# The mixer of an encoder layer: fp32 weight blocks against fp32r pieces in hand-ordered steps

## The chip, the cores and the metric

The kernel runs on one core of a Trainium2 chip. The metric is device time in microseconds (us), the median of three runs; a profiled execution of the same program supplies the trace. TensorE is called PE here, its weight loads PEld, VectorE DVE, ScalarE ACT, GpSimd POOL, and the queue that issues most transfers SP.

## The reference, cut to what matters

One layer over 256 tokens of width 2048. The mixer is everything up to `@ w_out`: a projection, a recurrent group (RWKV-7, both directions) and an attention group. The rest is a retrieval over 16384 single-neuron experts ("PEER").

```python
h = rmsnorm(x, norm1_w[l])
p = h @ w_in[l]                                  # 2048 x 5248
z_rwkv, q, k, v = jnp.split(p, IN_SPLITS, axis=-1)
y_rwkv = rwkv7_bidir(z_rwkv, ...)                # 16 heads x 64, delta-rule scans, two directions
y_attn = axial_gqa(q, k, v, q_norm_w[l], k_norm_w[l])   # 16 query heads, 4 key heads
x = x + jnp.concatenate([y_rwkv, y_attn], axis=-1) @ w_out[l]
x = x + peer_ffn(rmsnorm(x, norm2_w[l]), ...)    # queries, top-16 of 128 x 128 keys, all experts gated
out = rmsnorm(x, normf_w)
```

## The kernel before, in words

Activations stand transposed: 128 channels on the partitions, 256 tokens along the row. A block of weights is 128 input channels by 128 output channels, and a product of 2048 input channels is 16 matmuls into one PSUM tile `pj`.

The mixer and the rest use two ways of multiplying. The rest of the kernel (`query`, `up`, `down`) works in *pieces*. A piece is eight weight blocks (512 KB, tile `raw`); ACT rounds it to fp32r (`wH`), DVE or POOL subtracts to get what the rounding lost (`wL`), and PE multiplies the parts in the one-pass format fp32r. Pieces go through `load_piece`, `split_piece` and `go`, three pieces ahead of their use. There the instructions of each engine stand in the order in which the code issues them (`manual_schedule`).

The mixer before does not work that way. `proj` loads quarter blocks (`rw`, 256 KB) and multiplies them as plain fp32 with `xA`, the scaled tokens; `wout_block` does the same for the output projection, and `late` for its last part. Its order on the engines is set by a scheduler at build time from a list of parts, `ORDER`: U is the projection of a unit (four heads), P the operands of its scan (`prep`), I the inverse of 32 x 32 triangles (60 small DVE operations), M their merge on PE, C the scan's chain over four chunks, Q, K, V and A the attention, w the output projection. The operands go to DRAM (`D2`, `DV`) and come back as `PK` and `VV` for the chain.

So the program before is: first tokens, the mixer, eight `late` pieces, the queries and searches, and then the long stretch of `up` and `down` pieces.

Of the kernel before, what the change touches and what calls it, by code (L numbers as in the profile page):

```python
# [38 lines left out]
ORDER = ("U0 P0 U1 P1 U2 I0 P2 U3 Q4 M0 P3 V K Q0 Q3 A0 Q1 Q2 A1 W C0 I1 A2 M1 C1 A3 w2 w3 w0")  # L39
# [93 lines left out]

def body(tc, a, out, dbg={}):
    nc = tc.nc
    V, S, G, T = nc.vector, nc.scalar, nc.gpsimd, nc.tensor
# [51 lines left out]
    xy = actp.tile([128, 2, 16, 256], F, name="xy")  # L188
    xA, yA2 = xy[:, 0], xy[:, 1]
    yR, yT = yA2[:, 0:8], yA2[:, 8:16]  # L190
# [10 lines left out]

    stream = [pool("st")]

    def wload(src, n=4):
        raw = stream[-1].tile([128, n, 128], F, name="rw", bufs=8)
        nc.sync.dma_start(raw, src)
        return raw
# [26 lines left out]

# [7 lines left out]
    pss = bank("pt")[:, 0:2]  # L242
    pro = tc.tile_pool(name="pro", bufs=1, side="right")
    wp = pro.__enter__()
    xrs = [wp.tile([128, 4, 256], F, name="xr", bufs=4) for c in range(4)]
    for c in range(4):
        nc.sync.dma_start(xrs[c], a["xT"][:, 4 * c:4 * c + 4, :])
    nc.sync.dma_start(cst, a["cst"])
    for c in range(4):
        xr = xrs[c]  # L250
        tt(V if c < 2 else G, xA[:, 4 * c:4 * c + 4], xr,
           Pm("n1", 4 * c, 4)[:, :, None].to_broadcast([128, 4, 256]), OP.mult)
    for c in range(4):
        sq = wp.tile([128, 4, 256], F, name="xq", bufs=2)
        act(sq, xrs[c], AF.Square)
        sm = wp.tile([128, 256], F, name="xs", bufs=2)
        V.tensor_reduce(sm, sq.rearrange("p k t -> p t k"), axis=AX.X, op=OP.add)
        for b in range(2):
            mm(pss[:, b:b + 1], sm[:, b * 128:(b + 1) * 128], ones[:, 0:1], c + b == 0, c == 3)
    rstd = const.tile([128, 2, 1], F)  # L260
    rsqrt(wp, rstd[:, :, 0], pss, 2, 1.0 / 2048, 1e-6)
    psb = bank("pt")[:, :256]
    spread(psb, rstd.to_broadcast([128, 2, 128]))
    act(rstdb, psb)
    pro.__exit__(None, None, None)

    dr = pool("dr", 1, DRAM)
    ldp = pool("ldp", 1, side="right")
    rwc = pool("rwc", 1, side="right")
    at = pool("at", side="right")  # L270
    wk = pool("wk", 1)
    two = lambda p: p.rearrange("p (a b) -> p a b", a=2)

    def proj(n):
        p = pp.tile([128, 256], F, name="pj")
        for c in range(4):
# [5 lines left out]
    def headscale(pl, sq, scale, add, guard=None, tag="s2", bt="pr"):  # L282

        p = bank(bt)[:, :8].rearrange("p (b i h) -> p b i h", b=2, i=2)
        for b in range(2):
            for i in range(2):
                mm(p[:, b, i], sq[:, i, b * 128:(b + 1) * 128], bones[:, 0:128:64], b + i == 0, True)
        s1 = pl.tile([128, 8], F, name="s1")
        rsqrt(pl, s1, p.rearrange("p b i h -> p (b i h)"), 8, scale, add, guard)
        s2 = pl.tile([128, 8, 64], F, name=tag, bufs=2 if tag == "w2" else 1)  # L290
        V.tensor_copy(s2, s1[:, :, None].to_broadcast([128, 8, 64]))
        s2 = s2.rearrange("p (b i h) n -> p b i (h n)", b=2, i=2)
        p = bank(bt).rearrange("p (a b) -> p a b", a=2)
        for i in range(2):
            spread(p[:, i], s2[:, :, i])
        return p
# [958 lines left out]
```

## Time and profile before

| | us |
|---|---|
| median of three runs (2274.86 to 2278.29) | 2276.07 |
| profiled execution, its own time | 2277.42 |
| its span, first to last instruction | 2275.6 |
| mixer, from the first matmul with `xA` to the first `late` one | 14.1 to 635.5 |
| `late` pieces | 635.5 to 664.4 |
| queries, searches, experts, output | 664.4 to 2275.6 |

The span is what the trace covers; 1.8 us of the profiled time lie around it. PE is busy in 97% of the span, so the question in each stretch is what PE does there and at which clock, before what it waits for. A busy sum counts overlapping instructions once; the mean of one matmul contains its pipeline's depth, so the rate is read from starts, not from means.

### The profile page before, as it was taken

How to read it: one execution, taken by the hardware profiler on the slowest of the kernel's cores; microseconds unless marked ns; L12 is line 12 of the kernel's file. 1: busy time of each engine (PE TensorE's matmuls, PEld its weight loads, DVE VectorE, ACT ScalarE, POOL GpSimd, SP SyncE). 2: the span in 40 equal slices, each digit the busy share in tenths (PEclk: the TensorE clock that was granted, in tenths of full speed). 3: DMA queues.
4: the chain of work that ended last, by engine and by line, in shares of the span. 5: the costliest groups of instructions: out<-in, count | busy, mean ns of one | idle time of the engine just before them, and what ended most of it. 6: DMA issues, size and time to landing. Idle time of an engine off the chain costs nothing.

```text
span 2275.6 us, 33493 instructions
## 1 busy us (share of the span) xinstructions
PE 2214.7 (97%) x12790; PEld 1883.2 (83%) x12790; DVE 1223.4 (54%) x2556; ACT 961.8 (42%) x1479; POOL 823.6 (36%) x377
## 2 busy tenths in 40 slices
PE   7999799899999999999999999999999999999997
PEld 6888688787878889999888888888888888887886
DVE  3365875675367788887443352342533433456654
ACT  1121222323137755555544444444444444444443
POOL 0000000000027600000755555555555555556554
PEclk9999799699999999999999999999999999999999
DMA  5465364275455546666756666566566566676674
GB/s 196 148 188 174 127 196 146 82 240 174 138 183 170 174 160 221 213 209 215 240 189 205 203 194 209 190 203 212 187 211 205 185 211 205 194 229 212 207 209 133
DMA packets 188832, 431.50 MB, mean 190 GB/s; under 512 B 39680, under 2 KB 82304, under 8 KB 184448
## 3 DMA queue, kind: packets, MB, share of 16 engines
q1 hardware_dynamic: 177376, 409.96, 57.2%
q10 hardware_dynamic: 11296, 19.40, 2.5%
q8 instruction: 101, 1.65, 0.3%
q14 instruction: 59, 0.48, 0.1%
HBM read 391.55 MB, written 37.75 MB: 189 GB/s over the span
## 4 chain that ended last, share of the span: by engine, by line
PE 91%; DVE 5%; ACT 1%; DMA 1%; issue 1%; ACTq 0%; SPq 0%; DVEq 0%
PE pc L158 37%; PE pj L158 33%; PE pr L158 19%; PE pt L158 1%; DVE wL L164 1%; DVE oh L164 1%; ACT wH L161 0%; PE pr L532 0%; DMA VV<-V 0%; DVE pk L164 0%; DVE xy L164 0%; DVE hh L807 0%; DVE AK L164 0%; DVE h L164 0%; DVE rs L164 0%
## 5 line engine op out<-in xcount | busy, mean ns | idle before, releaser
L164 POOL TENSOR_TENSOR wL<-raw,wH 128x1024 fp32r<-128x1024 f32 x328 | 798.3, 2438 | 1018.5 <-ACT wH L161 1011.9
L161 ACT ACTIVATE wH<-raw 128x1024 fp32r<-128x1024 f32 x544 | 575.4, 1060 | 456.3 <-PE pc L158 282.8
L164 DVE TENSOR_TENSOR wL<-raw,wH 128x1024 fp32r<-128x1024 f32 x216 | 274.1, 1269 | 347.4 <-ACT wH L161 347.3
L158 PE MATMUL pr<-hh,wH 128*128 128x512 f32 x1152 | 409.3, 396 | 0.2 <-ACT wH L161 0.2
L158 PE MATMUL pj<-hh,wH 128*128 128x512 f32 x1152 | 408.0, 395 | 1.5 <-DVE hh L807 1.3
L158 PE MATMUL pc<-wH,aH 128*128 128x512 f32 x1024 | 406.7, 397 | 1.1 <-DVE acc L164 1.1
L158 PE MATMUL pc<-wH,aL 128*128 128x512 f32 x1024 | 404.8, 395 | 0.0
L158 PE MATMUL pc<-wL,aH 128*128 128x512 f32 x1024 | 402.0, 393 | 0.0
L158 PE MATMUL pj<-xy,rw 128*128 128x256 f32 x1664 | 382.6, 386 | 0.0
L158 PEld LDWEIGHTS pj<-xy,rw 128*128 128x128 f32 x1664 | 316.6, 193 | 49.6 <-issue 4.7
L158 PE MATMUL pr<-hh,wL 128*128 128x256 f32 x1152 | 323.1, 281 | 1.4 <-DVE wL L164 1.4
L158 PE MATMUL pj<-hh,wL 128*128 128x256 f32 x1152 | 322.1, 280 | 0.0
L158 PEld LDWEIGHTS pj<-hh,wH 128*128 128x128 f32 x1152 | 216.4, 188 | 48.4 <-DVE hh L807 2.0
L158 PEld LDWEIGHTS pr<-hh,wH 128*128 128x128 f32 x1152 | 217.2, 189 | 46.6 <-ACT wH L161 0.5
L158 PEld LDWEIGHTS pc<-wH,aL 128*128 128x128 f32 x1024 | 192.2, 188 | 48.3
L158 PEld LDWEIGHTS pc<-wL,aH 128*128 128x128 f32 x1024 | 192.3, 188 | 46.6
L158 PEld LDWEIGHTS pc<-wH,aH 128*128 128x128 f32 x1024 | 192.2, 188 | 46.1 <-DVE acc L164 1.5
L158 PEld LDWEIGHTS pr<-hh,wL 128*128 128x128 f32 x1152 | 217.2, 189 | 2.4 <-DVE wL L164 2.4
L158 PEld LDWEIGHTS pj<-hh,wL 128*128 128x128 f32 x1152 | 216.5, 188 | 0.4
L164 DVE TENSOR_TENSOR acc<-pc,acc 128x512 f32<-128x512 f32 x128 | 86.2, 688 | 131.6 <-PE pc L158 131.6
L504 POOL COPY vp<-zv 128x256 f32<-128x256 f32 x16 | 7.7, 482 | 307.2 <-PE pr L509 177.2
L161 ACT ACTIVATE gc<-pc 128x512 f32<-128x512 f32 x64 | 69.1, 1080 | 72.8 <-PE pc L158 72.8
(294 smaller groups left out, 1995.2 us busy)
## 6 DMA issues: line engine op xcount, KB each, us to landing
raw<-u SPq DMA_DIRECT2D x256, 512.0 KB, 4.1
raw<-v SPq DMA_DIRECT2D x256, 512.0 KB, 3.9
rw<-win SPq DMA_DIRECT2D x160, 256.0 KB, 2.8
PK<-D ACTq DMA_DIRECT2D x16, 1024.0 KB, 7.9
raw<-wpq SPq DMA_DIRECT2D x32, 512.0 KB, 4.3
gd<-gc SPq DMA_DIRECT2D x16, 1024.0 KB, 4.9
h<-gd SPq DMA_DIRECT2D x32, 512.0 KB, 6.9
D<-pk SPq DMA_DIRECT2D x16, 896.0 KB, 4.4
```

Of the source, the lines that this page charges most:

```text
L158: T.matmul(o, l, r, start=start, stop=stop, skip_group_check=True)
L161: S.activation(o, i, f, **kw)
L164: e.tensor_tensor(o, x, y, op=op)
L504: G.tensor_copy(vp[:, 1:5], c4(rev(zv[:, i], d)))
```

## The change

The mixer now works in the same pieces as the rest. Each piece is rounded on ACT and subtracted on DVE, and eight blocks cost 24 fp32r matmuls of 256 columns (`mm3`) instead of eight fp32 matmuls. The scheduler's order is replaced by one that is written out: a loop of steps. In a step the code issues first what the last step's piece left to do (`ends`), then one piece (`go(True)`: its rounding on ACT, its matmuls on PE), then one slice of every task (generators for heads, operands, inverses, bonuses, attention, chains), and at the end of the step the subtraction (`rest_pieces`). A task's slices are cut so that what one engine makes in a step is read by another in a later step. The last query blocks (32 to 37) and the gate's blocks stand behind the value blocks, and from there only every second step has a piece until all of them are used. Some work moves between engines: scalings and copies from DVE to ACT and POOL, the mask of the triangles to one operation ahead of the inverse.

```diff
+    def round_piece():
+        i = at_["split"]
+        H = stp.tile([128, 8, 128], R, name="wH", bufs=AHEAD + 1)
+        L = stp.tile([128, 8, 128], R, name="wL", bufs=AHEAD + 1)
+        act(H, raws[i])
+        hl[i] = (H, L)
+        at_["split"] += 1
+
+    def rest_pieces():
+        while at_["rest"] < at_["split"]:
+            i = at_["rest"]
+            H, L = hl[i]
+            tt(todo[i][2], L, raws.pop(i), H.bitcast(F), OP.subtract)
+            at_["rest"] += 1
...
+    def step(late=False):
+        now = list(ends)
+        ends.clear()
+        V.n = 0
+        for t in now:
+            next(t)
+        if late:
+            go(True)
+        for t in list(tasks):
+            tasks.remove(t)
+            if next(t, StopIteration) is not StopIteration:
+                tasks.append(t)
+            if V.n >= STEP:
+                break
+        tasks[:0] = now
...
-    def proj(n):
-        p = pp.tile([128, 256], F, name="pj")
-        for c in range(4):
-            W = wload(a["win"][n, :, 4 * c:4 * c + 4, :])
-            for k in range(4):
-                mm(p, W[:, k], xA[:, 4 * c + k], c + k == 0, c + k == 6)
-        return p
+    def x_block(n, c, evict):
+        def use(H, L):
+            if c == 0:
+                xp[n] = bank()[:, :256] if n == 24 else pj()
+            for k in range(8):
+                mm3(xp[n], H[:, k], L[:, k], xS[:, c + k, 0], xS[:, c + k, 1], c + k == 0, c + k == 15)
+            if c:
+                ends.append(evict(n, xp.pop(n)))
+        return from_rows(a["win"][n, :, c:c + 8, :]), use, V
...
-                V.tensor_scalar(sg, sg, 0.5, 0.5, op0=OP.mult, op1=OP.add)
-                V.tensor_scalar(av, av, 0.5, 0.5, op0=OP.mult, op1=OP.add)
+        G.tensor_scalar(sg, sg, 0.5, 0.5, op0=OP.mult, op1=OP.add)
+        G.tensor_scalar(av, av, 0.5, 0.5, op0=OP.mult, op1=OP.add)
+        G.tensor_scalar(a2, av, Pm("ka", j), ka1[:, j:j + 1], op0=OP.mult, op1=OP.add)
...
-    for q in ORDER.split():
-        parts[q[0]](int(q[1:] or 0))
+    tasks += [all_heads(), operand_tasks(), bonuses(), inverses(), reorder(), all_qk(), attend(), attended(), chains()]
+    slots = 0
+    while at_["use"] < NO or ("C", 1) not in done:
+        i = at_["use"]
+        ok = i < NO
...
+        if NX <= i < NA:
+            ok = "A" in done and bool(x2T)
+        elif NA <= i < NO:
+            ok = ("C", 0) in done
+        for u in range(2, 4):
+            if 8 + 12 * u < i < NX and ("P", u - 2) not in done:
+                ok = False
+        if NQ < i < NX and "at2" not in pools:
+            ok = False
+        slots += 1
+        if "at2" in pools and i < NX and slots % 2:
+            ok = False
+        step(ok)
+        rest_pieces()
```

In the order of the built program the loop has 129 steps. They are numbered from 1 here; 103 of them have a piece, and five pieces stand ahead of them. Two places show what moved.

On PE, inside the chain of the first two units; `VV`, `PK`, `X` and `N` are the chain's tiles, `zA`, `kW` and `pe` the attention's. Before, the scheduler laid groups of fp32 projection matmuls (`xy,rw`) between the slices:

```order
L158 MATMUL pr<-zA 128x256 x2
L158 MATMUL pr<-kW,zA 128x256 x2
L158 MATMUL pj<-xy,rw 128x256 x4
L158 MATMUL pc<-X,PK 64x64 x16
L376 MATMUL pr<-cst,pe 128x128 x4
L158 MATMUL pj<-xy,rw 128x256 x2
L158 MATMUL pr<-zA 128x256 x2
L158 MATMUL pj<-xy,rw 128x256 x6
L158 MATMUL pc<-VV,PK 64x64
L158 MATMUL pc<-PK,VV 64x64
```

In the changed program the same stretch, two steps of which the second has no piece, and the first rows of the next step's piece:

```order
L985 MATMUL pr<-cst,pe 128x128 x4
L177 MATMUL pr<-kW,zA_3716 128x256 x2
L177 MATMUL pc<-VV,PK 64x64 x16
L177 MATMUL pc<-PK,VV 64x64 x16
L177 MATMUL pt<-vA,pt 128x64 x4
L985 MATMUL pr<-cst,pe 128x128 x4
L177 MATMUL pr<-zA_3444,zA_3716 128x256 x2
L177 MATMUL pc<-VV,PK 64x64 x16
L177 MATMUL pj<-xy,wH 128x256 x2
L177 MATMUL pj<-xy,wL 128x256
```

The projection matmuls that lay between the slices now stand together, 24 at a time, and slices of two steps follow each other without one between them.

On DVE, inside the first inverse; the `h` rows are its small operations, `z` and `zv` belong to a projected block, `pk` to the scan's operands. Before:

```order
L164 TENSOR_TENSOR xy<-pr,zv 128x512
L164 TENSOR_TENSOR h_1545<-h_1545,h_1547 128x25x6
L164 TENSOR_TENSOR h_1547<-h_1545 128x168
L164 TENSOR_TENSOR h_1545<-h_1545,h_1547 128x24x7
L164 TENSOR_TENSOR h_1547<-h_1545 128x184
L164 TENSOR_TENSOR z<-pj,rstdb 128x256
L164 TENSOR_TENSOR h_1545<-h_1545,h_1547 128x23x8
L164 TENSOR_TENSOR h_1547<-h_1545 128x198
L408 SCALAR_TENSOR_TENSOR zv<-z,prm,zv 128x255
```

Now, with one step from the subtraction that ends the step before it to the operations of its operands:

```order
L149 TENSOR_TENSOR h_2479<-h_2477 128x198
L149 TENSOR_TENSOR h_2477<-h_2477,h_2479 128x9x22
L149 TENSOR_TENSOR wL<-raw,wH 128x1024
L149 SCALAR_TENSOR_TENSOR zr<-z,prm,zr 128x255 x2
L149 TENSOR_TENSOR pk_2661<-pc,cst 64x4x64
L149 TENSOR_TENSOR pk_2661<-pc,cst 128x4x64
L149 TENSOR_TENSOR pk_2661<-pc,cst 64x4x64
L149 TENSOR_TENSOR pk_2661<-pc,cst 128x4x64
L149 SCALAR_TENSOR_TENSOR cs_2945<-cst,sg_2809 128x256
L149 TENSOR_TENSOR av_2810<-kk,av_2810 128x256
L149 TENSOR_TENSOR a_2811<-zk,a_2811 128x256
```

A subtraction of 1024 columns (`wL<-raw,wH`) now stands in each step with a piece, and the inverse comes in groups of three pairs, one group a step.

## Rows read from the trace of the kernel before

**Rows 1.** Windows over the four stretches: busy us of each engine (instructions), clock, DMA, GB/s.

```profile
0.00:14.10 14.10, 1.70 (x8) 1.65 (x8) 9.06 (x13) 5.20 (x5) 4.94 (x6) 1.00 0.87 308
14.10:635.50 621.40, 593.31 (x4340) 505.10 (x4339) 349.70 (x967) 138.30 (x341) 20.30 (x40) 0.95 0.52 160
635.50:664.40 28.90, 28.76 (x136) 25.13 (x136) 17.90 (x28) 11.66 (x26) 3.71 (x2) 1.00 0.53 179
664.40:2275.60 1611.20, 1590.93 (x8308) 1351.33 (x8308) 846.74 (x1549) 806.68 (x1108) 794.60 (x330) 1.00 0.63 200
```

**Rows 2.** The page's chain that ended last, by engine.

```profile
PE 91%; DVE 5%; ACT 1%; DMA 1%; issue 1%; ACTq 0%; SPq 0%; DVEq 0%
```

**Rows 3.** The chain in order of time: start us, us, engine, line, instructions.

```profile
29.34 71.66 PE pj L158 x332
455.70 7.92 DMA VV<-V
1079.69 5.55 PE pj L158 x32
```

**Rows 4.** Timeline of PE in an `up` piece: start us, us, instruction.

```profile
1079.53 0.39 PE L158 MATMUL pj<-hh,wH 128*128 128x512 f32 x1
1079.76 0.28 PE L158 MATMUL pj<-hh,wL 128*128 128x256 f32 x1
1079.88 0.39 PE L158 MATMUL pj<-hh,wH 128*128 128x512 f32 x1
```

**Rows 5.** Groups of PE in the mixer, by form: busy us, mean ns, idle before.

```profile
L158 PE MATMUL pj<-xy,rw 128*128 128x256 f32 x1664 | 382.6, 386 | 0.0
L158 PE MATMUL pj<-rw,xy 128*128 128x256 f32 x64 | 15.1, 384 | 0.0
L158 PE MATMUL pr<-pk,AK 64*128 64x128 f32 x256 | 29.1, 332 | 11.2 <-DVE AK L164 11.2
L158 PE MATMUL pr<-tl,lo 96*128 96x256 f32 x64 | 18.5, 415 | 0.7 <-ACT pk L161 0.7
```

**Rows 6.** Windows of 4 us in the mixer; PEclk is the granted clock.

```profile
236.00:240.00 4.00, 0.00 (x0) 0.00 (x0) 3.84 (x10) 0.82 (x3) 0.95 (x1) 0.72 0.48 159
426.00:430.00 4.00, 4.00 (x14) 2.83 (x14) 2.75 (x8) 1.42 (x5) 0.00 (x0) 0.50 0.01 4
430.00:434.00 4.00, 4.00 (x14) 3.06 (x13) 0.00 (x0) 1.50 (x6) 0.00 (x0) 0.50 0.38 148
```

**Rows 7.** The page's groups of the roundings and of DVE's subtractions.

```profile
L161 ACT ACTIVATE wH<-raw 128x1024 fp32r<-128x1024 f32 x544 | 575.4, 1060 | 456.3 <-PE pc L158 282.8
L164 DVE TENSOR_TENSOR wL<-raw,wH 128x1024 fp32r<-128x1024 f32 x216 | 274.1, 1269 | 347.4 <-ACT wH L161 347.3
```

**Rows 8.** The page's group of one weight load.

```profile
L158 PEld LDWEIGHTS pj<-hh,wL 128*128 128x128 f32 x1152 | 216.5, 188 | 0.4
```

**Rows 9.** Timeline of DVE, neighbours that don't depend on each other.

```profile
258.24 0.41 DVE L164 TENSOR_TENSOR z<-pj,rstdb 128x256 f32<-128x256 f32 x1
258.57 0.48 DVE L408 SCALAR_TENSOR_TENSOR zr<-z,prm,zr 128x255 f32<-128x255 f32 x1
258.96 0.57 DVE L164 TENSOR_TENSOR Ld<-pr,cst 32x128 f32<-32x128 f32 x2
```

**Rows 10.** A POOL group of 256 columns with two operands.

```profile
L164 POOL TENSOR_TENSOR ks<-ks,av 128x256 f32<-128x256 f32 x8 | 7.6, 951 | 101.2 <-DVE av L164 101.2
```

**Rows 11.** DMA issues: KB each, median us from issue to landing.

```profile
PK<-D ACTq DMA_DIRECT2D x16, 1024.0 KB, 7.9
D<-pk SPq DMA_DIRECT2D x16, 896.0 KB, 4.4
```

**Rows 12.** Timeline of the start, ACT and PE.

```profile
5.72 1.06 ACT L161 ACTIVATE xq<-xr 128x1024 f32<-128x1024 f32 x1 [3.70 <-DMA xr<-xT]
14.25 2.05 PE L158 MATMUL pj<-xy,rw 128*128 128x256 f32 x4
```

**Rows 13.** Window over the first 57 us.

```profile
0.00:57.00 57.00, 44.60 (x199) 39.14 (x200) 20.90 (x42) 9.27 (x13) 4.94 (x6) 1.00 0.58 195
```

More of the change, by code (lines that the diff above doesn't have):

```diff
@@ L736, in body, with pj @@
[L736 to L738 removed]
+    def pj(w=256):
+        return pp.tile([128, w], F, name="pj")
+    two = lambda p: p.rearrange("p (a b) -> p a b", a=2)
+    stp = pool("st2")
     todo, raws, hl = [], {}, {}
[L742 removed]
+    at_ = {"load": 0, "split": 0, "rest": 0, "use": 0}
@@ L803, in use @@
                 act(sq[0][:, n % 4], x2(n), AF.Square)
[L804 removed]
+        return two_rows(m, 4), use, V
     def rest(n):
@@ new lines, in body, with operand_tasks @@
+    half, turn = set(), set()
+    fin = {}
+    def operand_tasks():
+        last = {}
+        for u in range(4):
+            while not (("head", u) in done and "tl" in done):
+                yield
+            for d in range(2):
+                los[u, d] = wk.tile([96, 2, 256], F, name=f"lo{d}")
+                nc.sync.dma_start(los[u, d], a["l2"][u][:, d::2])
+            for d in range(2):
+                for i in range(2):
+                    while i in last and last[i] not in half:
+                        yield
+                    last[i] = (u, i, d)
+                    tasks.append(operands(u, i, d))
+                    for _ in range(3):
+                        yield
@@ new lines, in body, with attend, attended @@
+    yA = {}
+    def attend():
+        while not ("at2" in pools and "V" in done and ("qk", 0) in done):
+            yield
+        for e in range(18):
+            g, hq = divmod(e, 4)
+            if e > 1:
+                values(e - 2)
+            if 0 < e < 17:
+                turned(e - 1)
+            if e < 16:
+                while ("qk", g) not in done:
+                    yield
+                scores(e)
+            yield
+    def attended():
+        for g in range(4):
+            while not (g in yA and yS):
+                yield
+            y = yA[g].rearrange("p b a n -> p b (a n)")
+            p = two(bank())
+            for j in range(2):
+                for b in range(2):
+                    T.transpose(p[:, j, b * 128:(b + 1) * 128], y[:, b, j * 128:(j + 1) * 128], ident)
+            s = slice(8 + 2 * g, 10 + 2 * g)
+            act(yS[0][:, s, 0], p)
+            tt(V, yS[0][:, s, 1], p, yS[0][:, s, 0].bitcast(F), OP.subtract)
+            yield
+        done.add("A")
@@ new lines, in chains, with reorder @@
+    def chains():
+        for k in range(2):
+            while not (("M", k) in done and "ck" in pools):
+                yield
+            yield from chain(k)
+    x2T = []
+    x2 = lambda n: x2T[n // 4][:, n % 4]
+    yS = []
+    def reorder():
+        while ("P", 3) not in done:
+            yield
+        close(wk)
+        pools["at2"] = pool("at2", side="right")
+        pools["rwc"] = pool("rwc", 1)
+        pools["ck"] = pool("ck")
+        while ("M", 1) not in done:
+            yield
+        for k in range(4):
+            x2T.append(hole(k, [128, 4, 256]))
+            nc.sync.dma_start(x2T[k], a["xT"][:, 4 * k:4 * k + 4])
```

1064 lines of the change are left out of this document (603 added, 461 removed).

## The prediction

> **What bounds the kernel now.** I looked first at the span in four stretches [rows 1]. PE is busy in 593.31 of 621.40 us of the mixer and in nearly all of the 1611.20 us behind the late pieces, and it holds 91% of the chain that ended last [rows 2]. So the kernel is one long queue on PE, and a change in the mixer is worth what it takes out of the 621.40 us. The parts behind it have the same pieces as before and keep their 1611.20 us.
>
> Then I took the mixer's time apart. In the chain a run of fp32 projection matmuls has 332 records in 71.66 us [rows 3], 0.216 us each. There are 1664 + 64 records [rows 5], two to a matmul of 256 columns: 864 matmuls of 0.432 us, 373 us. In pieces of eight that is 108 pieces of 3.45 us. The rest of PE's busy time is 593 - 373 = 220 us: heads, operands, merges, chains, attention. Part of that is clock: the mean granted clock of the stretch is 0.95 [rows 1], which at the two levels 2.4 and 1.2 GHz means some 62 us at 1.2 GHz, and up to 31 us lost. Full-clock work outside the projections is thus near 189 us, and 28 us are idle. The mixer before is 373 of projections, 189 of small work, 31 of clock, 28 of idle.
>
> **The change part by part.** *Pieces.* An `up` piece has a matmul of 512 columns and one of 256 for each block; their starts are 0.23 and 0.12 us apart [rows 4], and two pieces took 5.55 us [rows 3]. Three matmuls of 256 columns move the same 768 columns. I take 0.117 us each, 2.81 us a piece, since 5.55 / 2 = 2.78. That is 0.64 us under an fp32 piece; over 108 pieces 69 us.
>
> The Trainium skill (FP8 and Floating Point Precision, section TensorE Precision Notes) says that true fp32 takes four passes through the array, high and low halves against each other. The trace's two records of 0.216 us for 256 columns agree. Writing three of the four out would by that rule cost three quarters of 3.45, 2.59 us a piece, and gain 24 us more than the starts do; the starts decide.
>
> *New work on other engines.* Each piece asks 1.06 us of ACT and 1.27 us of DVE [rows 7]. Neighbours on DVE overlap by 0.08 us (starts 0.33 us apart for an operation of 0.41) [rows 9], so a subtraction holds DVE for about 1.15 us: 108 x 1.15 = 124 us. DVE was busy for 349.70 us of the mixer [rows 1], but scalings, copies and half-height operations have left it. I went through the 129 steps in the program's order and added up each engine's work, with DVE at 0.33 us for 256 columns, 0.60 for 512, 0.40 for the shift's operations and 0.12 for the small ones, ACT at 0.36 and 0.55, and PE at 2.81 us for a piece, 0.43 for a 96-row matmul, 0.21 for one of `pk,AK`, 0.06 for the chain's. POOL gets 48 scalings of 256 columns; its nearest row is 0.95 us for two operands [rows 10], three in a row below one step, and the two `yield`s behind them cover that. As an example, a step within the first inverse: PE 2.81 + four sums of a head 0.9 = 3.7; DVE subtraction 1.13, eviction 0.33, thirteen small operations 1.5, five of the operands 1.65, six of the inverse 1.7 = 6.3. By steps, in us:
>
> - 1 to 42 (units 0 to 2): PE 143, DVE 108, ACT 90
> - 43 to 68 (last unit, first inverse, values): PE 112, DVE 99, ACT 83
> - 69 to 105 (half of the steps without a piece; second inverse, first chain, attention): PE 122, DVE 86, ACT 90
> - 106 to 129 (second chain, output): PE 92, DVE 56, ACT 40
> - together: PE 468, DVE 349, ACT 303
>
> PE remains the engine with the most work, but not in every step. If each step lasted as long as its busiest engine and nothing were shared between neighbours, the sum would be 543 us. If two neighbours share (the code lets PE run about two steps ahead of DVE, since a slice reads what was made two `yield`s earlier, and a piece is rounded three ahead), it is 510; if three do, 493. I take pairs, 510.
>
> *Waits that the steps don't hide.* The first chunk of a chain is loaded by ACT's queue, 7.9 us to landing, and behind it lie the operands' stores, 4.4 us [rows 11]; the trace of before has such a wait on the chain too, 7.92 us [rows 3]. One step's piece covers 2.8 us. I put 7 us for the first chain and 6 for the second, in whose steps 104 and 105 there is no piece. In the steps without a piece the attention's scores wait for a maximum on DVE and two exponentials on ACT within one step: some 1 us in eight steps, 8 us. The values take both `pj` buffers at once: 3 us. PE's clock: it fell to 0.5 after a window in which PE did nothing, and stayed there for windows in which PE was busy throughout with small matmuls [rows 6]. Now full pieces stand in 103 of 129 steps, and only 69 to 105 look like those windows; I put 6 us there (0 to 31). Steps 1 to 129: 510 + 7 + 6 + 8 + 3 + 6 = 540.
>
> *The start.* The first matmul with the tokens began at 14.25 us [rows 12]. The first tokens landed by 5.72 us; scaling, rounding and subtraction then take about 4 us, so PE begins near 10, but five pieces, the tokens and the constants are 5.1 MB, at 195 GB/s [rows 13] 26 us, and the fifth must be rounded and subtracted. The loop starts near 29 us (26 to 32).
>
> *The late pieces.* PE falls from 28.9 to 23 us; DVE had 17.90 us [rows 1] and gets five subtractions, 24 us, and the two alternate. I take 27, a gain of 2.
>
> *Sum.* The late pieces begin at 29 + 540 = 569 us instead of 635.5, 66.5 earlier; with the 2 us, 68.5. From the profiled 2277.4 that is 2209, and the profiled execution lies 1.35 us over the median: 2208 for the median.
>
> **The rivals.** *Steps without sharing.* DVE or ACT sets each step in which it has most to do, as if the steps ran one by one: 543 + 24 + 15 of clock = 582, late pieces at 611, total 2250. For it: one order on each engine, so that a slice which waits holds up everything behind it, the next subtraction too. Against: three pieces of lead.
>
> *Full sharing.* Steps even out over three and the chunks' loads stay hidden: 493 + 5, total 2166. For it: in the `up` stretches, where everything is written in order too, PE has no gap.
>
> *The clock falls and stays (slower than before).* In steps 43 to 105 PE has 234 us of work, against 276 us of step time by pairs. If much of it ran at 1.2 GHz, 42 us of the extra would go into idle time. To use up the whole gain of 68 us, 110 us of extra work, nearly half of the 234, must run at that level. At three quarters it is 176 - 42 = 134 more, 2343. For it: small matmuls alone did not bring the clock back [rows 6]. Against: before, 62 us in all.
>
> *Weight loads that don't overlap.* A load has a record of 188 ns [rows 8]. If it ran after the matmul before it instead of beside it, a piece would be 24 x (0.117 + 0.188) = 7.3 us, 3.9 more than now, and the time near 2690. Against it: the next matmul starts 0.12 us after one of 256 columns, less than a load's record [rows 4]. The Trainium skill (TensorE: Matmul & The Clock Gate, Part 3, The mechanism) says that loads overlap matmuls in flight only when their row groups differ, which would be this case, since every block uses all rows; the starts contradict it.
>
> *The change does nothing.* The new order's idle time equals the pieces' gain: 28 + 31 us of idle and clock before would have to become 127.
>
> **How the numbers follow.** The forecast, 2166 to 2241 around 2208, has 0.55; steps without sharing, 2241 to 2268, 0.20; full sharing, down to 2150, 0.13; no change 0.03; the clock 0.07; the loads 0.02. Two runs of this kernel can be told apart from about 0.2%, 4.6 us. So faster 0.88, same 0.03, slower 0.09. The range for 8 in 10 goes from 2160 to 2266: below by full sharing, above by single steps with some clock.
>
> **What would show it.** Starts of `xy,wH` and `xy,wL` 0.117 us apart and pieces of 2.81 us would show the first term; the late pieces' first matmul near 569 us the sum; DVE busy for 350 to 400 us until then, with PE's waits for `wL`, `AK` and `pk` in steps 43 to 68, the sharing; a gap of 6 to 7 us before the first `VV,PK` matmul of each chain the loads; a clock of 0.97 or more in the mixer the 6 us. It is wrong if matmuls of 256 columns in a row lie further apart than beside one of 512, if PE waits for DVE in most steps, or if the granted clock is 0.5 through the steps without pieces.

## The result and the profile after

The changed kernel takes 2291.51 us (median of four runs, 2291.26 to 2293.98), the kernel before, run beside it, 2277.18: a ratio of 1.0066, 95% interval 1.0049 to 1.0084. It is slower by 15 us; the forecast was 2208, faster by 69, with a range up to 2266. It was wrong in sign and by 83 us.

The windows of the profile after, by stretch (us, then busy us and count of PE, weight loads, DVE, ACT, POOL, then granted clock, DMA share, GB/s), against [rows 1]: the first pieces start at 9.4 us, the loop's first piece at 33.6, the late pieces at 637.1, the queries at 673.8.

```profile
9.40:33.60 24.20, 20.68 (x136) 20.22 (x137) 23.36 (x37) 15.50 (x24) 0.00 (x0) 0.93 0.69 244
33.60:637.10 603.50, 527.76 (x5139) 487.80 (x5138) 394.43 (x861) 281.65 (x584) 41.18 (x82) 0.90 0.56 162
637.10:673.80 36.70, 27.68 (x203) 27.00 (x201) 23.62 (x34) 16.43 (x31) 3.76 (x2) 0.91 0.32 101
673.80:2289.20 1615.40, 1596.58 (x8308) 1358.13 (x8308) 840.01 (x1550) 806.24 (x1108) 792.15 (x330) 1.00 0.63 199
```

The late pieces begin 1.6 us later than before instead of 66.5 us earlier. In the loop PE is busy for 527.76 of 603.50 us at a mean clock of 0.90; before it was 593.31 of 621.40 at 0.95. The page's chain by engine, against [rows 2], has PE down from 91% to 84% and DVE up from 5% to 8%:

```profile
PE 84%; DVE 8%; ACT 3%; DMA 2%; issue 2%; SPq 0%; ACTq 0%; DVEq 0%
```

The pieces themselves did what the first term said. A timeline of PE inside one, against [rows 4]: the starts of neighbours lie 0.12 us apart, whether the weights change between them or not, and a piece takes 2.88 us where the forecast had 2.81 and fp32 3.45.

```profile
136.97 0.40 PE L177 MATMUL pj<-xy,wH 128*128 128x256 f32 x2
137.21 0.28 PE L177 MATMUL pj<-xy,wL 128*128 128x256 f32 x1
137.33 0.40 PE L177 MATMUL pj<-xy,wH 128*128 128x256 f32 x2
```

So where did it go? I laid PE's records over the trace's records of the granted clock and counted a microsecond of busy time at 1.2 GHz as half a microsecond of work at 2.4. PE was busy at the lower level for 56 us of the mixer before and for 91 us of the loop after. That splits each stretch into work at full clock, idle time and what the lower clock cost:

| us | before | after | difference |
|---|---|---|---|
| to the first matmul with the tokens | 14.1 | 9.4 | -5 |
| PE's work at full clock (after: 14 in five pieces ahead of the loop, 482 in it) | 565 | 496 | -69 |
| rest of the 24 us of those five pieces | | 10 | +10 |
| PE idle in the mixer (after: loop) | 28 | 76 | +48 |
| cost of the lower clock there | 28 | 45 | +17 |
| late pieces | 28.9 | 36.7 | +8 |
| behind them | 1611.2 | 1615.4 | +4 |
| sum (span 2275.6, now 2289.2) | | | +13 |

Of the 10 us beside the first five pieces, PE was idle for only 3.5; for the rest their matmuls start 0.21 us apart instead of 0.12, until 15.4 us and from 29.2 to 32.5, and the norm's small sums lie between.

So PE's work fell by about the 69 us of the forecast, of which the pieces are 62 (108 x 0.57). The match is in part luck: some 2.5 of the 565 us are the lower rate of the first matmuls before, ahead of the first record of the clock, and the 14 leave out 2 us of the norm's sums, so the fall is 65 to 69. Waits and clock ate all of it. The three longest kinds of PE's waits in the loop (total us, times, longest):

```profile
PE pr L177 <- DMA lo<-l: 18.2, 4, 6.8
PE pc L177 <- DMA VV<-V: 18.0, 4, 11.3
PE pc L177 <- ACT Ld L180: 12.3, 6, 5.3
```

They make up 48.5 us, and in each the order written by hand has something too late.

*`lo`.* The code issues the weights of the low-rank maps only one step ahead of the slice that reads them, on SP's queue behind another operand's store (`V<-Vm`). SP runs late itself: between 110 and 134 us it waited 5.3 us for a `raw` buffer that DVE's subtraction frees. So it came to `lo` at 126.50, when PE had ended the piece of the reading step at 126.2. PE's timeline and SP's, at the start of unit 1's operands; the issue at 126.50 lands 5 us later:

```profile
131.57 2.04 PE L177 MATMUL pr<-tl,lo 96*128 96x256 f32 x4 [5.37 <-DMA lo<-l]
```

```profile
125.38 1.02 SPq L790 DMA_DIRECT2D V<-Vm  x1
126.50 1.32 SPq L821 DMA_DIRECT2D lo<-l  x2
```

*`Ld`.* The PSUM banks (`pc`) of one operand are read two steps later, by ACT, and ACT stands in its own order behind a scaling (`zk`) that waits for DVE, which has the inverse's rows and a subtraction ahead. PE, ACT and DVE around one such wait:

```profile
237.62 2.60 PE L177 MATMUL pc<-pk,AK 64*128 64x128 f32 x15 [5.29 <-ACT Ld L180]
```

```profile
235.52 0.51 ACT L180 ACTIVATE zk<-z,der 128x256 f32<-128x256 f32 x1 [4.95 <-DVE z L149]
235.94 1.04 ACT L180 ACTIVATE wH<-raw 128x1024 fp32r<-128x1024 f32 x1
236.88 0.25 ACT L180 ACTIVATE L<-pc 32x128 f32<-32x128 f32 x1
```

```profile
233.93 1.22 DVE L149 TENSOR_TENSOR wL<-raw,wH 128x1024 fp32r<-128x1024 f32 x1
235.07 0.42 DVE L149 TENSOR_TENSOR z<-pj,rstdb 128x256 f32<-128x256 f32 x1
```

*`VV`.* The second chain's first chunk is issued on ACT's queue behind the last epilogue operation of the first chain (`xy<-L`), and PE waits 11.35 us:

```profile
521.63 0.63 ACT L180 ACTIVATE xy<-L 128x512 fp32r<-128x512 f32 x1 [2.08 <-DVE L L149]
521.63 0.33 ACTq L1044 DMA_DIRECT2D PK<-D  x1
```

```profile
527.55 0.44 PE L177 MATMUL pc<-VV,PK 64*64 64x64 f32 x2 [11.35 <-DMA VV<-V]
```

In the late pieces DVE and ACT alternate: DVE's subtraction waits for ACT's rounding, the piece's sum waits behind it and a reduction, and PE for the sum. DVE, then PE:

```profile
648.38 1.23 DVE L149 TENSOR_TENSOR wL<-raw,wH 128x1024 fp32r<-128x1024 f32 x1 [1.83 <-ACT wH L180]
649.52 0.48 DVE L149 SCALAR_TENSOR_TENSOR hh<-h,prm,hh 128x256 fp32r<-128x256 f32 x1
649.91 1.88 DVE L149 TENSOR_REDUCE sm<-sq 128x256 f32<-128x1024 f32 x1
651.71 0.41 DVE L149 TENSOR_TENSOR h<-pj,h 128x256 f32<-128x256 f32 x1
```

```profile
652.27 0.48 PE L177 MATMUL pj<-xy,wH 128*128 128x256 f32 x2 [3.35 <-DVE h L149]
```

### The profile page after: what moved, and what is told of

Read it like the earlier page. It is cut to its first block, busy times and chain, and to the rows that moved or that the text cites. A ratio compares the mean times of both kernels' runs of the same rounds, so it can differ in the third digit from the quotient of the medians.

```text
span 2289.2 us, 35699 instructions
## 1 busy us (share of the span) xinstructions
PE 2172.7 (95%) x13782; PEld 1893.2 (83%) x13782; DVE 1283.7 (56%) x2491; ACT 1123.7 (49%) x1752; POOL 837.3 (37%) x417
## 4 chain that ended last, share of the span: by engine, by line
PE 84%; DVE 8%; ACT 3%; DMA 2%; issue 2%; SPq 0%; ACTq 0%; DVEq 0%
PE pc L177 37%; PE pj L177 26%; PE pr L177 20%; DVE wL L149 2%; ACT wH L180 1%; DVE rs L149 1%; DMA lo<-l 1%; DVE h L149 1%; DMA VV<-V 1%; DVE oh L149 1%; PE pt L177 0%; DMA D<-pk 0%; DVE pk L149 0%; DVE hh L149 0%; DVE xy L149 0%
## 5 line engine op out<-in xcount | busy, mean ns | idle before, releaser
L180 ACT ACTIVATE wH<-raw 128x1024 fp32r<-128x1024 f32 x660 | 696.3, 1058 | 482.5 <-PE pc L177 273.6
L149 DVE TENSOR_TENSOR wL<-raw,wH 128x1024 fp32r<-128x1024 f32 x332 | 411.8, 1241 | 405.8 <-ACT wH L180 405.5
L177 PE MATMUL pj<-xy,wH 128*128 128x256 f32 x1632 | 331.4, 304 | 19.6 <-ACT wH L180 9.5
L177 PEld LDWEIGHTS pj<-xy,wH 128*128 128x128 f32 x1632 | 275.8, 206 | 29.3 <-issue 13.9
L177 PE MATMUL pj<-xy,wL 128*128 128x256 f32 x816 | 241.1, 295 | 0.5 <-DVE wL L149 0.5
L177 PEld LDWEIGHTS pj<-xy,wL 128*128 128x128 f32 x816 | 167.6, 205 | 0.9 <-DVE wL L149 0.9
```

The source lines that it names most:

```text
L149: return f(*args, **kw)
L177: T.matmul(o, l, r, start=start, stop=stop, skip_group_check=True)
L180: S.activation(o, i, f, **kw)
```

## The experiments

Two theories stood at first. W: PE is the bound, and loses its time in single late things, each followed by a stretch at the lower clock. S: DVE and ACT set the steps, and PE's waits only show it. C was a third, that the clock falls by itself in thin steps. Each run stands beside runs of the kernel before on its own chip. The last column takes the ratio of the changed kernel, 1.0066, off that of the run and multiplies by 2277; the two intervals make it uncertain by about 5 us.

| run | median us | ratio to before, 95% interval | against the changed kernel, us |
|---|---|---|---|
| e1_lo | 2277.59 | 0.9994 (0.9984 to 1.0003) | -16 |
| e2_chunk | 2292.44 | 1.0064 (1.0047 to 1.0081) | 0 |
| e3_full | 2288.39 | 1.0041 (1.0026 to 1.0055) | -6 |
| e4_late | 2285.86 | 1.0043 (1.0027 to 1.0060) | -5 |
| e5_irate | 2293.02 | 1.0066 (1.0044 to 1.0087) | 0 |
| e7_two | 2253.99 | 0.9893 (0.9876 to 0.9909) | -39 |
| e8_fp32 | 2330.73 | 1.0223 (1.0204 to 1.0243) | +36 |
| e9_mix | 2271.80 | 0.9967 (0.9955 to 0.9979) | -23 |
| e10_fill | 2288.62 | 1.0044 (1.0027 to 1.0060) | -5 |
| e11_pool | 2310.70 | 1.0137 (1.0120 to 1.0154) | +16 |
| e12_chunk2 | 2289.38 | 1.0051 (1.0034 to 1.0068) | -3 |
| e13_nosub | 2268.95 | 0.9955 (0.9938 to 0.9971) | -25 |
| e14_three | 2268.64 | 0.9956 (0.9940 to 0.9973) | -25 |
| e15_yield | 2260.32 | 0.9932 (0.9915 to 0.9949) | -30 |
| e16_full | 2265.71 | 0.9938 (0.9920 to 0.9956) | -29 |
| e17_yield2 | 2259.82 | 0.9913 (0.9897 to 0.9930) | -35 |

### What a microsecond of PE or DVE is worth

**e7_two.** One of three matmuls of a block is left out in 104 pieces.

```diff
+    def mm2(ps, sH, sL, mH, start, stop):
+        mm(ps, sH, mH, start, False)
+        mm(ps, sL, mH, False, stop)
...
-                mm3(xp[n], H[:, k], L[:, k], xS[:, c + k, 0], xS[:, c + k, 1], c + k == 0, c + k == 15)
+                mm2(xp[n], H[:, k], L[:, k], xS[:, c + k, 0], c + k == 0, c + k == 15)
```

> The changed kernel with two of the three matmuls of a block in 104 of the mixer's pieces: the product of the rounded weights with the rest of the activations is left out. Rounding, subtraction, transfers and order are the same, and PE has 104 x 8 x 0.12 = 100 us less to do. Theory W (PE's queue is the bound outside the waits): 60 to 90 us of them come back, 2201 to 2231. Theory S (steps as long as their longest engine, in which PE is often not that): 20 to 45 us, 2246 to 2271. Theory C: PE thinner, so the clock is lower than 0.90 in the mixer and less than 40 us come back.

**e8_fp32.** One fp32 matmul for each block again; the order, the rounding and the subtraction kept.

```diff
+    def mm1(ps, s_, m, start, stop):
+        mm(ps, s_.bitcast(F), m.bitcast(F), start, stop)
...
-                mm3(p, H[:, k], L[:, k], yS[0][:, 8 + k, 0], yS[0][:, 8 + k, 1], k == 0, k == 7)
+                mm1(p, H[:, k], yS[0][:, 8 + k, 0], k == 0, k == 7)
```

> The changed kernel in its own order, with the pieces' arithmetic undone: each block of the 108 mixer pieces is one fp32 matmul (of the rounded weights with the rounded activations) instead of three fp32r ones, and the products with the rests are left out; rounding, subtraction, transfers and steps stay. PE gets 108 x (3.45 - 2.88) = 62 us more to do. Theory W (PE sets the time outside single waits): nearly all of it shows, 2340 to 2354. Theory S (much of it falls into PE's idle time in the steps; with 100 us taken away only 40 came back): 2315 to 2335. Either way the time over that of the kernel before is the price of the written-out order alone; if that price were small, under 15 us (2292 or less), the pieces gained nothing on PE.

**e13_nosub.** No subtraction in the mixer's pieces.

```diff
-        L = stp.tile([128, 8, 128], R, name="wL", bufs=AHEAD + 1)
+        L = H if i < NO else stp.tile([128, 8, 128], R, name="wL", bufs=AHEAD + 1)
...
-            tt(todo[i][2], L, raws.pop(i), H.bitcast(F), OP.subtract)
+            raw = raws.pop(i)
+            if i >= NO:
+                tt(todo[i][2], L, raw, H.bitcast(F), OP.subtract)
```

> The changed kernel without the subtraction in the mixer's pieces: the rest of the weights is left out, and the rounded weights stand in its place in the third matmul, so PE, ACT, transfers and steps have the same work and DVE has 103 x 1.22 = 126 us less to do in the loop (394 becomes 268 of 603 us). Theory S (DVE's new work sets steps, above all 43 to 68, where DVE is busy for 107 of 130.7 us): 20 to 50 us of it come back, 2241 to 2271. Theory W (single waits for loads and banks, in which DVE has no part): 2284 to 2294, and DVE's new work lay beside PE's at no cost.

The windows over the loop of the three, in that order:

```profile
33.70:597.20 563.50, 446.21 (x4346) 401.35 (x4345) 392.71 (x861) 281.57 (x584) 43.19 (x82) 0.87 0.59 172
```

```profile
36.80:675.80 639.00, 577.91 (x4314) 488.05 (x4313) 395.70 (x861) 281.98 (x584) 46.50 (x82) 0.93 0.52 152
```

```profile
32.90:617.50 584.60, 517.59 (x5138) 480.14 (x5137) 283.56 (x761) 281.49 (x584) 37.05 (x82) 0.92 0.56 166
```

With PE's work down by 100 us (PE's busy time fell by 82), 39 come back and idle time grows to 117 us. With 62 us more, 36 show and idle time shrinks to 61. With DVE relieved of 111 us of busy time, 25 come back. By their numbers all three fall in S's ranges; e7 also meets C's sign, a clock under 0.90 (it is 0.87) and less than 40 us back. But DVE returns a fifth of what it is relieved of, so S doesn't hold alone either: a microsecond of PE's work is worth 0.4 to 0.6 here, one of DVE's 0.2. e8 also splits the change, though not as cleanly as its expectation says. Against the kernel before, the written-out order with fp32 blocks costs 51 us (1.0223), and the three fp32r matmuls for one of fp32 give back 36. The 51 are not the order's alone, since e8 keeps the rounding on ACT and the subtraction on DVE, which the kernel before has not, and the subtraction alone is worth 25 us in e13. What order and pieces each cost by themselves no run shows.

### Late things, one by one

**e1_lo.** Each `lo` loaded when its tile is free.

```diff
+        def lo_load(u, d):
+            los[u, d] = wk.tile([96, 2, 256], F, name=f"lo{d}")
+            nc.sync.dma_start(los[u, d], a["l2"][u][:, d::2])
+
+        for d in range(2):
+            lo_load(0, d)
...
-            for d in range(2):
-                los[u, d] = wk.tile([96, 2, 256], F, name=f"lo{d}")
-                nc.sync.dma_start(los[u, d], a["l2"][u][:, d::2])
             for d in range(2):
                 for i in range(2):
...
+                if u < 3:
+                    lo_load(u + 1, d)
```

> The changed kernel with the 192 KB blocks `lo` of the low-rank maps loaded earlier: each half for the next unit as soon as both operands of the unit before that read it have begun, instead of in the step in which the first matmul reads it. Nothing else moves. Theory W (PE is the bound, and loses time in single waits for things that are late, each followed by a stretch at the lower clock): PE's four waits for `lo` in the trace, 18.2 us, go, and with them some 10 us of the four stretches at 1.2 GHz that begin at 70.0, 128.0, 192.9 and 268.0 us; the time is about 2263 us (2255 to 2275). Theory S (DVE and ACT set each step, as if steps ran one by one, and PE's waits are only where that shows): the wait moves to the next operand or eviction and the time stays within 2284 to 2293. Theory C (the clock falls in thin stretches whatever the waits): only the waits go, 2273.

All waits for `lo` went, and 16 of their 18 us with them, so S fails here. Set against the runs beside it the time is 2275, nearer C's 2273 than W's 2263; the first late piece moved from 637.1 to 621.2 us. (The old load stood one step ahead of its reader, not in the same step as the expectation says.) PE's waits for `Ld` rose from 12.3 to 16.7 us, and of 17.6 us won by piece 44, 3.6 were lost again by piece 68, in the first inverse. The cost of the clock fell by 2 us, not 10.

**e2_chunk** and **e12_chunk2.** The chunk loads elsewhere; the second without moving the first chain, and with

```diff
-            if c < 3:
-                nxt = chunk_load(us, c + 1)
             pX = p8()
...
             act(X, pX)
+            if c < 3:
+                nxt = chunk_load(us, c + 1)
...
-        while k and ("C", 0) not in done:
-            yield
+        if not k:
+            while ("M", 1) not in done:
+                yield
+            yield
+            first[1] = chunk_load((2, 3), 0)
```

> The changed kernel with the first chunk of each scan chain loaded at another time: that of the second pair of units before the first pair's epilogue instead of behind it, that of the first pair three steps later than now (when the memory it lies in has been released) and with two steps in front of its first use instead of one. Theory W: PE's waits for `VV` (18.0 us, one of 11.3) go, and some 5 us of the slow clock behind the second, so about 2268 us (2260 to 2280); the first pair's later start costs nothing, since its results wait for the gate anyway. Theory S: the attention's and epilogue's steps are as long as before, 2284 to 2293. Theory C: 2274.

> The changed kernel with the second chain's first chunk loaded before the first chain's epilogue instead of behind it, as in the other run on the chunks, but with the first chain left where it is, and with the load of each following chunk issued behind ACT's eviction of `X` instead of ahead of it (there the eviction had to wait for four transfers to be issued on ACT's queue, and PE for the eviction). Theory W: the wait of 11.3 us shrinks to some 3, since the epilogue on ACT and DVE ends at 522 us instead of the load at 527.5, and with it the 20 us of slow clock: 2277 to 2284. If the attention and the epilogue set the end of this stretch as they did in the other run: 2288 to 2294.

e2 came out as S forecast, e12 at its second expectation. In e2 the wait for `VV` is gone and another stands in its place; PE and, on ACT, what is ahead of `X`:

```profile
532.23 1.98 PE L177 MATMUL pc<-X,PK 64*64 64x64 f32 x32 [8.66 <-ACT X L180]
```

```profile
527.92 0.63 ACT L180 ACTIVATE xy<-L 128x512 fp32r<-128x512 f32 x1 [2.09 <-DVE L L149]
...
529.71 0.61 ACTq L1044 DMA_DIRECT2D PK<-D  x1
530.35 1.18 ACTq L1046 DMA_DIRECT2D VV<-V  x2
531.58 0.60 ACT L180 ACTIVATE X<-pc 128x512 f32<-128x512 f32 x1 [3.03 <-issue]
```

The epilogue and the issue of the next chunk's six transfers hold ACT until 531.58. With these behind `X` (e12) the wait is 5.5 us and the first late piece comes at 632.0 instead of 637.1, but the median can't be told from that of the changed kernel. The 11.3 us were thus mostly not to be had: ACT's and DVE's epilogue ends at nearly the same time.

**e4_late.**

```diff
-        return two_rows(m, 4), use, V
+        return two_rows(m, 4), use, G if m > 2 else V
```

> The changed kernel with the subtractions of the last five `late` pieces on POOL instead of DVE. In the late pieces DVE and ACT alternate (a piece's subtraction, its sums, the rounding of its tokens and the next piece's rounding), and PE waits 9.2 us for them. If that alternation sets the stretch, it shrinks from 36.7 to about 29 us and the time is 2284 (2281 to 2287); if POOL's slower subtraction comes late instead, 2289 to 2296.

As the alternation says: 5 us by the medians, about as much as they are uncertain, and in the trace the time from the start of the first late piece to that of the eighth shrinks from 31.9 to 25.7 us.

**e5_irate.**

```diff
-IRATE = (3, 4)
+IRATE = (2, 4)
```

> The changed kernel with two instead of three rows of the first 32 x 32 inverse in each step: its 32 slices spread over 16 steps instead of 11, and DVE has about 0.8 us less to do in each. Theory S (in these steps DVE's sum is longer than PE's, and ACT's evictions of `Ld` wait behind it): the two waits of 5.3 and 4.2 us at 232 and 254 us shrink, and the clock that fell with them, so 2280 (2276 to 2285). Theory W (the waits there come from the PSUM banks alone): no difference, 2288 to 2294.

Piece 60 came 14.2 us earlier, piece 68 0.3 later: the `Ld` waits shrank from 9.5 to 5.9 us, but between pieces 60 and 64, where the rows that were put off are now made, 12 us were lost again. By its number this is W. By the pieces it is S for the inverse's rows: DVE is busy for 107 of 131 us in these steps either way, and a row costs its time in whichever step it stands. But the sum of DVE's work is not the bound there. In e13, with DVE busy for 81 us instead of 107, the stretch from piece 44 to piece 68 takes 124.3 us instead of 130.7:

```profile
199.10:323.40 124.30, 112.52 (x1091) 105.32 (x1089) 81.16 (x217) 74.39 (x166) 16.91 (x37) 0.93 0.64 176
```

**e14_three**, **e15_yield**, **e17_yield2.** The edits of e1, e4 and e12 together; then with one `yield` in place of two between the operands' matmuls and the reading of their banks; then the same between the exponentials and the scaled operands.

> Three of the single edits together, all arithmetic kept: `lo` loaded early (-14 alone), the last subtractions of the late pieces on POOL (-6), the second chain's first chunk before the epilogue and the next chunks behind the eviction of `X` (-2). If they act on different waits, as their places say, they add up: 2270 (2266 to 2274). If each takes the other's gain: 2275 or more.

> The same three edits, and the operands' PSUM banks read one step after they are written instead of two, so that they are free a step earlier for the next operand and the loop has two steps fewer. If PE's 12 waits for `Ld` come from banks that are held too long: 6 to 12 us under the run with the three edits alone, near 2261. If DVE and ACT, which read them, are what is late (theory S), the same as that run within 3 us; if PE's matmuls now come too late for them, more.

> The kernel with the three edits and the banks read a step earlier, and in it the scaled operands made one step after the exponentials instead of two: again two steps fewer and everything behind an operand sooner. If the two-step distance is what delays (the banks' reading was): 3 to 8 us less, 2252 to 2257. If DVE now waits for ACT's exponentials inside its order: 2260 to 2268.

The three add up as forecast (2268.64 for 2270). Reading the banks a step earlier gives another 8 us by the medians (their intervals touch), and the loop in the trace shrinks from 583.9 to 573.3 us, so held banks were part of the `Ld` waits: those of `pc` sum to 18.4 us in e14 and are gone in e15, where one of `pr` takes 6.1. The second `yield` gave nothing that can be told. The loop of e15:

```profile
34.80:608.10 573.30, 514.33 (x5140) 477.05 (x5139) 395.52 (x861) 282.95 (x584) 39.89 (x82) 0.93 0.57 170
```

e15 and e17 beat both kernels of the change, at 0.9932 and 0.9913 of the time before. So what e15 moves is enough for the sign: 15 us slower becomes 15 us faster.

### The clock

**e10_fill.**

```diff
         p = bank()
+        for _ in range(36 if u and not (d or i) else 0):
+            mm(p[:, :256], xS[:, 0, 0, 0:128], xS[:, 1, 0])
```

> The changed kernel with filler matmuls whose result nobody reads, put on PE in front of four waits and nowhere else: 36 of 256 columns (some 4.3 us) ahead of the first `tl,lo` matmul of units 1 to 3, where PE waited 5.4, 6.8 and 4.2 us for `lo`, and 80 (some 9.6 us) ahead of the second chain's first `VV,PK` matmul, where it waited 11.3. All waits stay as they are, PE just isn't idle in them. Theory W, its part on the clock (an idle PE is what makes the clock fall): the stretches at 1.2 GHz that begin at 128.0, 192.9, 268.0 and 517.1 us (44 us together) go or shrink, and the time falls by 8 to 18 us, to 2274 to 2284. Theory C (the clock falls because of what PE does in these steps, not because it is idle): the stretches stay, and the time is 2290 to 2296, a little more than without the fillers.

Windows around two of the four places, the changed kernel and then this one (the granted clock is the third number from the end):

```profile
126.00:133.00 7.00, 1.63 (x6) 1.19 (x5) 4.52 (x11) 0.41 (x1) 0.00 (x0) 0.65 1.03 283
190.00:198.00 8.00, 1.15 (x4) 0.89 (x4) 6.08 (x12) 2.05 (x8) 0.00 (x0) 0.69 0.93 246
```

```profile
124.00:133.00 9.00, 6.00 (x42) 5.69 (x42) 4.83 (x12) 1.84 (x5) 0.78 (x2) 0.92 0.96 265
188.00:197.00 9.00, 6.97 (x55) 6.66 (x55) 5.83 (x12) 3.61 (x12) 0.88 (x3) 1.00 0.88 235
```

With PE busy in the same waits the clock stays up: 0.92 and 1.00 instead of 0.65 and 0.69, and 0.86 instead of 0.57 in a third, from 514 to 538 us. The fillers didn't run over: behind them PE still waited 3.0, 2.0 and 1.4 us for `lo` and 2.7 for `VV`. So in these places it is the idle PE that makes it fall. The median gains 3 us, no more than can be told from nothing, where W forecast 8 to 18. There was less to win than 18: PE worked at the lower level for only 22 us in these four stretches, which cost 11 of the loop's 45.

C is not refuted by this. Among the steps without a piece the clock also falls where PE hardly waits. Three windows of the changed kernel:

```profile
435.00:442.00 7.00, 7.00 (x41) 4.93 (x38) 5.49 (x11) 4.20 (x10) 0.00 (x0) 1.00 0.76 292
442.00:446.00 4.00, 4.00 (x22) 4.00 (x22) 3.28 (x22) 1.95 (x6) 0.00 (x0) 0.57 0.25 90
500.00:510.00 10.00, 10.00 (x42) 8.26 (x41) 3.98 (x8) 4.52 (x14) 0.41 (x1) 0.51 0.15 49
```

It fell at 442.2 with PE busy throughout the 7 us before, and at 500.2 after waits of 0.7 us in all. In the 6 us before each, PE ran matmuls of the attention, at 442 of the first chain's epilogue too, with no piece between them. No run took these falls apart.

### The thin steps, and POOL

**e3_full**, **e9_mix**, **e16_full.** No rule of every second step; a mixture; the same with the waits gone.

```diff
-        if "at2" in pools and i < NX and slots % 2:
-            ok = False
```

> The changed kernel without the rule that from the value blocks on only every second step has a piece: the loop then has six steps fewer, 15 pieces stand in neighbouring steps, and some 13 steps in a row behind them have none. Theory W: the stretch from step 69 to the end of the attention took 194 us in the trace for 122 us of PE work; with 14 steps of about 6.5 us and 14 of about 4.5, and the second chain's first chunk loaded under the attention, it takes some 155, so 2255 us (2240 to 2275). Theory S: six steps fewer of about 5 us, 2262. Theory C: the steps without pieces, now in a row, all run at 1.2 GHz, and the time stays at 2280 or more.

> Several edits together, all of the reference's arithmetic kept: `lo` loaded early, no rule of every second step, the attention's share of the output projection in two halves of eight pieces so that the first half fills the steps in which the last heads are still attended, the slower first inverse, and the late subtractions on POOL. The loop has 113 steps instead of 127, 10 of them without a piece instead of 25. Theory S (steps without a piece are idle and slow-clocked time on PE, so fewer of them count): the stretch from step 69 to the last attention piece takes 194 + 16 pieces now and shrinks by 30 to 45 us; with 14 for `lo`, 8 for the late pieces and 5 to 10 for the inverse the time is 2225 (2205 to 2245). If the single edits share one cause, so that each takes the gain of the others: 2255 to 2275.

> The kernel with the three edits and the banks read a step earlier, and in it a piece in every step behind the value blocks, with the attention's output pieces in halves: 111 steps, 9 without a piece, instead of 125 with 24. If steps without a piece are what costs, now that the loads no longer stand in their way: 10 to 25 us under that kernel, 2235 to 2250. If the work of PE and the chain of the attention set this stretch whatever stands between, as the mixture of edits seemed to show: 2257 to 2266.

e3 came out at the number of C (2280 or more): where its steps without a piece stand in a row, from 463.6 to 546.3 us, the granted clock is 0.75 and PE is busy for 63 of 83 us. But filling these steps doesn't help, so they are not what costs by themselves. In e9, with 113 steps instead of 127 in the loop proper, the stretch from piece 69 to piece 92 took 214.8 us; in the changed kernel 216.9. e9's 23 us are about those of e1 and e4, as its second expectation had it. e16, with the waits gone, is no faster than e15, its second expectation too.

**e11_pool.**

```diff
-        return from_rows(a["win"][n, :, c:c + 8, :]), use, V
+        return from_rows(a["win"][n, :, c:c + 8, :]), use, G if c else V
```

> The changed kernel with half of the mixer's subtractions on POOL (the second piece of each projection block, every second output piece), which was busy for 41 of 603 us there. A subtraction takes 2.43 us on POOL in the later stretches and 1.24 on DVE. Theory S (DVE sets steps 43 to 68, where it is busy for 107 of 130.7 us): 13 subtractions fewer there, 15 us, of which 8 to 15 show, and some more around the operands of the first units: 2274 to 2284. If waits for loads and PSUM banks set these steps: 2287 to 2294. If POOL's subtraction comes too late for PE: above 2294.

Slower, the third of the expectations by its number, but PE waited for POOL's `wL` only once, 3.9 us. Another reason is told in the last section.

## Why the prediction was wrong, point by point

- *Pieces, 2.81 us each, -69.* Right in mechanism, and nearly in size: 2.88 us, 62 us for 108 pieces, and PE's work fell by 65 to 69 in all. Weight loads didn't get in the way.
- *The sum of PE's work, 468* (its four parts add up to 469). 482 measured in the loop, 14 too little; 7 of them are the 0.07 us of 103 pieces.
- *Sharing by pairs (42) and waits (24), together 66 us of idle PE.* 76 measured, so the size was nearly right, but its parts weren't. The first chunks were put at 7 and 6 us; they took 3.6 and 11.3, though most of the 11.3 could not be won (e2, e12). Neither `lo` (18.2 us) nor the banks (12.3) was in the list: I looked at each step's sums and at transfers of the chain, and not for a transfer issued only a step ahead of its reader, which the code showed, or for how late its queue runs.
- *Clock, 6 us (0 to 31).* The term that failed by most: 45. "Only 69 to 105 look like those windows" was the wrong step, in two ways. Up to piece 68, where full pieces stand in most steps and nothing was put, the clock fell eight times, each time in or behind a wait of 1.4 to 6.8 us on PE, at a cost of 20 us. And from there to the first output piece, the stretch that was named, it cost 22, partly with PE busy throughout; the last 4 lie behind it. The stretches of the loop (to piece 44, to piece 68, to the first output piece, to the late ones):

```profile
33.60:208.30 174.70, 153.28 (x1237) 147.04 (x1236) 117.39 (x243) 91.83 (x200) 21.28 (x43) 0.91 0.60 169
208.30:339.00 130.70, 113.77 (x1091) 105.89 (x1089) 106.99 (x241) 74.36 (x166) 18.10 (x37) 0.92 0.63 166
339.00:533.40 194.40, 160.15 (x1650) 138.64 (x1650) 109.53 (x268) 78.80 (x172) 1.81 (x2) 0.84 0.47 142
533.40:637.10 103.70, 100.57 (x1165) 96.23 (x1164) 60.53 (x110) 36.66 (x48) 0.00 (x0) 0.96 0.57 181
```

- *Loop start, 29 us.* 33.6: 4.6 late, with 3.5 us of waits and the slow first matmuls, which were in no term. *Late pieces, 27 us.* 36.7, 10 over: I saw that DVE and ACT alternate and took 4 us for it. *Behind them* 1615.4 for 1611.2, not followed up.

The differences, 4.6 + 14 + 10 + 39 + 10 + 4, make the 82 us. Under them lies one error that the sum hides: I added PE's work, its waits and its clock as if each microsecond counted in full, since PE held 91% of the chain before. In the new order it counts for about half (e7, e8), for waits move from one thing to the next when one is removed (e2, e5; in e1 16 of 18 us stayed won). Whether the 45 us that the clock cost could be won back stays open: e10 kept it up where it cost 11 and gained 3, within its uncertainty. So 39 of the 82 are where the time shows and not a cause that was shown. e15 says the same from the other side. With the late things moved, PE's idle time in its loop is 59 us, under the forecast's 66, and of the 49 us that its span still lies over the forecast, 28 are the clock (34 for 6).

Of the signs that the prediction named, the starts and DVE's busy time (394 us) came as said. The late pieces (637 for 569) and the clock (0.90 for 0.97) did not, and PE waited for `lo`, `VV` and `Ld` rather than for `wL`, `AK` and `pk`.

Of the rivals, "steps without sharing" had the right kind for the inverse's rows in steps 43 to 68 (e5), but not for DVE's sum: 26 us less of it gave back 6 there (e13). The idle time that it gave PE, 99 us (543 - 468 + 24), lies above the 76 measured. "The change does nothing" named the condition that came true: idle time and clock would have to grow from 59 to 127. They are 131, with the 10 us beside the first pieces, and the late pieces did the rest. It had 0.03, because I set step sums without any latency against the idle time of a scheduler's order. "The clock falls and stays" was half right: it fell 16 times in the loop, for 3.4 to 20.5 us each, and never stayed. "Weight loads that don't overlap" was refuted by the 0.12 us between starts.

What stays open: 27 of the 76 us of idle time lie in waits under 2.5 us, which no run took apart; nor did one take apart the falls of the clock with PE busy; and e15 frees banks and saves two steps at once, so its 8 us aren't split between the two.

## What to carry to other kernels

When an order written by hand replaces a scheduler's, price the order by itself: the arithmetic may gain nearly what it should on its engine (here 62 us, of which 36 showed in the time) and the order, with the work that the arithmetic puts on other engines, lose more (51). A sum of engine times per step is a lower bound; read the order of each queue for a transfer issued only a step ahead of its reader, for a bank held over two steps, and for a load queued behind an unrelated eviction, and put those first. Removing a wait is worth its length only if the next thing is not nearly as late: test two waits alone and together before adding them.

## What the runs showed of the hardware

In e11 an operation of DVE with both inputs in SBUF waited for a running POOL subtraction to end. POOL and DVE at its first such place: `tl<-z,prm,tl` takes 2.61 us instead of the 0.48 of the same operation two rows below, and ends 0.28 us behind POOL's.

```profile
39.91 2.53 POOL L183 TENSOR_TENSOR wL<-raw,wH 128x1024 fp32r<-128x1024 f32 x1 [8.54 <-ACT wH L180]
```

```profile
40.11 2.61 DVE L149 SCALAR_TENSOR_TENSOR tl<-z,prm,tl 128x255 f32<-128x255 f32 x1
...
42.76 0.48 DVE L149 SCALAR_TENSOR_TENSOR tl<-z,prm,tl 128x255 f32<-128x255 f32 x1
```

The groups of DVE in the loop, the changed kernel and then e11: a scan from SBUF goes from 680 to 1425 ns, an operation that reads PSUM stays at 417. That is why 48 subtractions fewer left DVE busy for 403 us instead of 394.

```profile
L149 DVE TENSOR_TENSOR pk<-pc,cst 64x256 f32<-64x256 f32 x32 | 13.3, 417 | 0.4
...
L149 DVE TENSOR_TENSOR_SCAN cs<-cst,sg 128x256 f32<-128x256 f32 x16 | 10.9, 680 | 0.0
```

```profile
L149 DVE TENSOR_TENSOR_SCAN cs<-cst,sg 128x256 f32<-128x256 f32 x16 | 22.8, 1425 | 0.5 <-POOL sg L731 0.5
...
L149 DVE TENSOR_TENSOR pk<-pc,cst 64x256 f32<-64x256 f32 x32 | 13.3, 417 | 0.3
```

The Trainium skill (SBUF — State Buffer, section SBUF: two separate sides) says that a DVE operation with two SBUF inputs and a POOL operation that reads SBUF take a shared pair of ports as an exclusive lock, which the first holds for its whole instruction. The rows agree, 2.61 against 0.48 us.

The runs show one thing more: fp32r matmuls with a weight load each start 0.12 us apart for 256 columns, without a 512-column one between them, though a load's record is 188 ns long [rows 8].
